# Four attention heads' 32 sample queries on the four quarters of the partitions, with one softmax for the four

## The chip, the cores and the metric

The kernel runs on one core of one Trainium2 chip. The metric is device time in microseconds (us) for one execution of the whole program; a lower time is better.

## What is computed

Two layers of a small model are run over 288 tokens: a prompt of 256 and, apart from it, a sample of 32 new tokens with its own states and caches. Layer 0 mixes tokens by retention and gated linear attention, layer 1 by band attention; each is followed by a gated feed-forward net with a short convolution. Everything is float32. The change is in layer 1's attention, 16 heads of width 128:

```python
def band_attention_prompt(q, k, v, rel_bias):      # chunks of 64 queries
    ...
        s = jnp.einsum('bihd,bjhd->bhij', qn, ks) * scale + bias[None]
        s = jnp.where(valid[None, None, None, :], s, NEG_INF)
        p = jax.nn.softmax(s, axis=-1)
        return jnp.einsum('bhij,bjhd->bihd', p, vs)
...
def band_attention_sample(q, k_new, v_new, k_cache, v_cache, rel_bias):
    ks = jnp.concatenate([k_cache.astype(jnp.float32), k_new], axis=1)
    vs = jnp.concatenate([v_cache.astype(jnp.float32), v_new], axis=1)
    ...
    s = jnp.einsum('bihd,bjhd->bhij', q, ks) * (q.shape[-1] ** -0.5) + bias[None]
    p = jax.nn.softmax(s, axis=-1)
    return jnp.einsum('bhij,bjhd->bihd', p, vs)
```

For each head the sample has 32 queries against 288 keys: 256 from the cache and 32 of its own.

## The kernel before

Activations stand with features on the 128 partitions and the 288 tokens in the columns (256 of the prompt, then 32 of the sample). A projection, `project`, makes one tile of 128 outputs: for each of 16 blocks of 128 inputs it runs three matmuls of 288 columns in float32r (lines 79, 80, 81), since each float32 operand is split into a high and a low part. The weights come in chunks of 8 blocks (512 KB) on SyncE's queue; ScalarE rounds a chunk to its high part `wh` (line 57), VectorE subtracts it to give `wl` (line 58). There are four buffers for a chunk as loaded and three each for `wh` and `wl`.

An attention head is a generator, `att_head`, of five steps:

1. project q and k of the head (two projections);
2. project v;
3. scores and softmax. The prompt's scores take two matmuls (lines 681, 682), the sample's two more with only 32 output partitions (684 against its own keys, 685 against the cache's); v is turned to tokens on partitions by three transposes (689, 690, 691, the last one for the sample). VectorE adds the biases and takes the maxima, ScalarE takes exponentials, VectorE divides; all of it once for each of the prompt's two halves and once for the sample (tile `ass`, 32 partitions by 288);
4. transpose the probabilities: 721, 722, 726 for the prompt, 723, 727, 728 for the sample's cache halves and own keys;
5. the product with v: 734 and 735 for the prompt, 736, 737 and 738 for the sample, all into one PSUM tile, which is split into `bh` and `bl`, the operands of the output projection.

`chain` interleaves the heads: while head h does its steps 4 and 5, head h+1 does 1, 2 and 3, so the instructions of a head's step 5 and of the next head's step 3 stand next to each other on TensorE, after the next head's v projection. Within this order a list scheduler places the instructions; each engine then runs its own list in order. The attention's small loads and stores (caches, biases, k and v out) go through GpSimd's queue (POOL). A plain float32 matmul, such as all those of steps 3 to 5, becomes two instructions on TensorE; a transpose becomes one.

Of the kernel before, what the change touches and what calls it, by code (L numbers as in the profile page):

```python
# [5 lines left out]
F32 = mybir.dt.float32  # L6
F32R = mybir.dt.float32r
U32 = mybir.dt.uint32
AF = mybir.ActivationFunctionType
# [20 lines left out]
NEG = -1e30  # L30
QA, KA, VA, GA, QB, KB, VB, GB = 0, 8, 16, 24, 32, 36, 40, 48


class Trunk:
# [15 lines left out]
    def weights(self, src, n, lo=False):  # L50
        """n k-tiles of 128 rows: the float32 tile as the sum of two float32r tiles."""
        nc = self.nc
        w = self.wp.tile([P, WCH, P], F32, name="w", tag="w", bufs=4)[:, :n, :]
        h = self.wp.tile([P, WCH, P], F32R, name="wh", tag="wh", bufs=3)[:, :n, :]
        l = self.wp.tile([P, WCH, P], F32R, name="wl", tag="wl", bufs=3)[:, :n, :]
        nc.sync.dma_start(w, src)
        nc.scalar.copy(h, w)  # L57
        nc.vector.tensor_tensor(l, w, h.bitcast(F32), op=ALU.subtract)  # L58
        return h, l

    def project(self, src, xh, xl, nk, k0=0, chunks=None, part=None, ps=None):
        """PSUM [128 outputs, T]: the product over nk k-tiles of float32 operands split in two."""
# [20 lines left out]
    def first_project(self, src, x):  # L83
        """As project, while the input is loaded and the first norm's operands come about."""
# [14 lines left out]
    def first_squares(self, x):  # L99
        """The sum of squares, in the place of x."""  # L100
# [16 lines left out]
    def rsqrt(self, out, ms_ps, inv_n, p=P, n=T, tag="rs"):  # L117
        """out = (ms_ps * inv_n + eps) ** -0.5"""
# [37 lines left out]
    def norm_stat(self):  # L156
        """R [128, T]: each token's 1 / rms, on all partitions; worked out with tokens on partitions."""
# [22 lines left out]
    def run(self, ctx):  # L180
# [11 lines left out]
        self.bh = [bp.tile([P, T], F32R, name=f"bh{k}", tag=f"bh{k}") for k in range(KD)]  # L192
        self.bl = [bp.tile([P, T], F32R, name=f"bl{k}", tag=f"bl{k}") for k in range(KD)]
        with self.tc.tile_pool(name="ab", bufs=1) as pool:
            self.ab_mixer(pool, *sums)
        with self.tc.tile_pool(name="x", bufs=1) as xp:
# [7 lines left out]
            with self.tc.tile_pool(name="c", bufs=2) as pool:  # L204
                self.chain(
                    [self.att_head(pool, hd) for hd in range(H_ATT)], 3,
# [31 lines left out]
        # The gate's low-rank features: both parts of the weights side by side in one tile's columns  # L238
        # (their sum is taken in the product with w2, which stands twice).
# [19 lines left out]
    def out_proj(self, w, n, chunks):  # L259
        """x += o @ w, and the next norm's start."""  # L260
# [83 lines left out]
    def head_out(self, pool, o, gates, hd, g):  # L344
        """Gated, normalised head output into the split operands of w_out; o: two PSUM tiles."""
# [18 lines left out]
    def to_tokens(self, pool, feats, name, width, scale=None, bufs=1):  # L364
        """[128 tokens, 3, width] from feature-major [128, T] tiles."""
# [13 lines left out]
    def scaled(self, pool, ps, name, scale=None, rev=False):  # L379
        nc = self.nc  # L380
        z = pool.tile([P, T], F32, name=name, tag=name)
        if scale is None:
            nc.vector.tensor_tensor(z[:, ::-1] if rev else z, ps, self.R, op=ALU.mult)
# [4 lines left out]
    def ab_mixer(self, pool, k0, q0, lo_ps):  # L388
# [19 lines left out]
        def gates():  # L408
            """log sigmoid of the gates, tokens on partitions (its 1/16 is in the level matrices)."""
# [39 lines left out]
    def gla_head(self, pool, hd, w, la, lvl, masks, eyem, hg, first):  # L449
# [14 lines left out]
        # E[:, l]: decays to and from the middle of each token's block of level l. Slot 7: level 256  # L464
        # (tile 0 before, tile 1 behind the middle), and from the sample's start; slot 8: to the end.
# [31 lines left out]
        # Scores, transposed: each pair of tokens belongs to the one level whose middle parts them.  # L497
# [66 lines left out]
        # States.  # L564
# [89 lines left out]

    def att_head(self, pool, hd):
# [4 lines left out]
        kc = pool.tile([P, TP], F32, name="kc", tag="kc")  # L660
        vc = pool.tile([P, 2, P], F32, name="vc", tag="vc")
        nc.gpsimd.dma_start(kc, a["cache_k"][hd])
# [3 lines left out]
        bias_s = pool.tile([TS, T], F32, name="bias_s", tag="bias_s")  # L666
        rel = a["rel"]
        toep = lambda n, m, c: bass.AP(rel.tensor, rel.offset + hd * RELW + c, [[1, n], [1, m]])
        nc.gpsimd.dma_start(bias, toep(P, TP, 256 - 127))
        nc.gpsimd.dma_start(bias_s, toep(TS, T, 256 - 31))  # L670
        nc.gpsimd.memset(bias[:64, :64], NEG)

        q = self.scaled(pool, self.input_product(w[hd]), "aq", scale)
        k = self.scaled(pool, self.input_product(w[16 + hd]), "ak", rev=True)
        nc.gpsimd.dma_start(a["k_out"][hd], k)
        yield
        v = self.scaled(pool, self.input_product(w[32 + hd]), "av", rev=True)
# [3 lines left out]
        nc.tensor.matmul(ps[:, :P], lhsT=q[:, :P], rhs=k[:, TS + P :], start=True, stop=True)  # L681
        nc.tensor.matmul(ps[:, P:384], lhsT=q[:, P:TP], rhs=k[:, TS:], start=True, stop=True)  # L682
        pss = self.mm()[:TS]
# [3 lines left out]
        vt = pool.tile([P, 3, P], F32, name="avt", tag="avt")  # L687
        pv = self.mm()
        nc.tensor.transpose(pv[:, :P], v[:, TS : TS + P], self.ident)
        nc.tensor.transpose(pv[:, P:TP], v[:, TS + P :], self.ident)  # L690
        nc.tensor.transpose(pv[:TS, TP : TP + P], v[:, :TS], self.ident)
        nc.scalar.copy(vt[:, 0:2, :], pv[:, :TP].rearrange("p (t d) -> p t d", t=2))
        nc.scalar.copy(vt[:TS, 2, :], pv[:TS, TP : TP + P])

        s = pool.tile([P, 384], F32, name="as", tag="as")
        ss = pool.tile([TS, T], F32, name="ass", tag="ass")
        mx = pool.tile([P, 3], F32, name="mx", tag="mx")
        sm = pool.tile([P, 3], F32, name="sm", tag="sm")
        nc.vector.memset(mx, 0.0)
        nc.vector.memset(sm, 1.0)  # L700
# [3 lines left out]
        parts = ((s[:, :P], P, 0), (s[:, P:], P, 1), (ss, TS, 2))  # L704
        for x, n, i in parts:
            nc.vector.tensor_reduce(mx[:n, i : i + 1], x, axis=X, op=ALU.max, negate=True)
        for x, n, i in parts:
            nc.scalar.activation(x, x, AF.Exp, bias=mx[:n, i : i + 1], accum_out=sm[:n, i : i + 1])
        nc.vector.reciprocal(sm, sm)
        for x, n, i in parts:  # L710
            nc.vector.tensor_scalar(x, x, sm[:n, i : i + 1], None, op0=ALU.mult)
# [149 lines left out]
```

## Time and profile before

| | us |
|---|---|
| median of three timed runs (2761.59 to 2763.56) | 2762.46 |
| span of the profiled execution, first to last instruction | 2760.1 |
| TensorE busy in that span | 2732.1 (99%) |
| VectorE busy | 1572.3 (57%) |
| ScalarE busy | 1123.9 (41%) |
| GpSimd busy | 126.5 (5%) |

The profile is of one execution, for which the span is given and no other time; the median of the timed runs is 2.4 us longer than that span, and this part lies outside the first and last instruction. Matmuls are pipelined: the duration of one runs from its start to its modelled end and overlaps the next, so what a matmul costs TensorE is read from the distance to the next, which is what the view of the chain that ended last prints.

### The profile page before, as it was taken

Reading aid. Unit: us, or ns where it says so; the run is one execution under the profiler, and the core shown is the slowest. Engines: PE = TensorE matmul, PEld = TensorE weight load, DVE = VectorE, ACT = ScalarE, POOL = GpSimd, SP = SyncE. Lnnn points to the kernel's source line nnn. Section 1 sums busy time; section 2 is a strip of 40 time slices with the busy share of each in tenths; the row PEclk is TensorE's granted clock in tenths of the full one; section 3 lists DMA queues with packets and bytes.
Section 4 is the critical chain, followed back from the end, with each engine's and each line's share of the span. In section 5 each row is a group of like instructions: output and inputs, shape, how many; then the busy total and the mean of one; then the engine's idle time right before and its main releaser. Section 6 shows DMA issues by size and latency. Waiting matters only on the chain.

```text
span 2760.1 us, 49198 instructions
## 1 busy us (share of the span) xinstructions
PE 2732.1 (99%) x20340; PEld 2686.5 (97%) x20340; DVE 1572.3 (57%) x2536; ACT 1123.9 (41%) x1538; POOL 126.5 (5%) x440
## 2 busy tenths in 40 slices
PE   8999999999999999999999999999999999999997
PEld 7999999999999999999999999999999999999997
DVE  6566555666665456665555555556666544666544
ACT  7444343443343333334444333344333333433443
POOL 1000000000000000000011111100000000000000
PEclk9999999999999999999999999999999999999999
DMA  5334444545555555555555555544555555555553
GB/s 198 117 131 142 152 157 149 192 162 166 168 167 161 168 168 165 167 168 162 166 182 170 166 165 165 163 156 162 166 165 166 162 167 168 168 166 166 163 167 125
DMA packets 126546, 448.84 MB, mean 163 GB/s; under 512 B 15562, under 2 KB 15754, under 8 KB 126320
## 3 DMA queue, kind: packets, MB, share of 16 engines
q1 hardware_dynamic: 119520, 427.15, 48.6%
q0 software_dynamic: 6656, 18.49, 2.1%
q8 instruction: 159, 2.61, 0.4%
q14 instruction: 67, 0.55, 0.1%
q10 hardware_dynamic: 144, 0.04, 0.0%
HBM read 435.22 MB, written 10.40 MB: 161 GB/s over the span
## 4 chain that ended last, share of the span: by engine, by line
PE 97%; ACT 1%; DVE 1%; DMA 1%; issue 0%; SPq 0%; DVEq 0%; ACTq 0%
PE acc L80 31%; PE acc L79 30%; PE acc L81 30%; PE mm L520 1%; DMA x_in<-in_xT 0%; PE mm L372 0%; PE mm L643 0%; ACT wh L57 0%; PE mm L682 0%; PE mm L685 0%; PE mm L734 0%; PE mm L681 0%; DVE wl L58 0%; DVE y L334 0%; PE mm L738 0%
## 5 line engine op out<-in xcount | busy, mean ns | idle before, releaser
L57 ACT CAST wh<-w 128x1024 fp32r<-128x1024 f32 (+1 forms) x816 | 843.7, 1034 | 1505.9 <-PE acc L80 1209.0
L58 DVE TENSOR_TENSOR wl<-w,wh 128x1024 fp32r<-128x1024 f32 (+1 forms) x816 | 981.0, 1203 | 761.7 <-ACT wh L57 761.4
L79 PE MATMUL acc<-xh,wh 128*128 128x288 f32 x4480 | 1323.0, 295 | 8.6 <-ACT wh L57 7.7
L81 PE MATMUL acc<-xh,wl 128*128 128x288 f32 x4480 | 1323.5, 295 | 1.3 <-DVE wl L58 1.3
L80 PE MATMUL acc<-xl,wh 128*128 128x288 f32 x4480 | 1324.0, 296 | 0.0
L79 PEld LDWEIGHTS acc<-xh,wh 128*128 128x128 f32 x4480 | 843.2, 188 | 13.3 <-ACT wh L57 7.9
L81 PEld LDWEIGHTS acc<-xh,wl 128*128 128x128 f32 x4480 | 842.6, 188 | 2.8 <-DVE wl L58 2.1
L80 PEld LDWEIGHTS acc<-xl,wh 128*128 128x128 f32 x4480 | 843.0, 188 | 2.0 <-issue 1.0
L79 PE MATMUL acc<-bh,wh 128*128 128x288 f32 x1920 | 567.1, 296 | 0.4 <-ACT wh L57 0.4
L80 PE MATMUL acc<-bl,wh 128*128 128x288 f32 x1920 | 566.3, 295 | 0.0
L81 PE MATMUL acc<-bh,wl 128*128 128x288 f32 x1920 | 565.0, 294 | 0.0
L79 PEld LDWEIGHTS acc<-bh,wh 128*128 128x128 f32 x1920 | 360.1, 188 | 1.3 <-ACT wh L57 0.6
L81 PEld LDWEIGHTS acc<-bh,wl 128*128 128x128 f32 x1920 | 361.2, 188 | 0.0
L80 PEld LDWEIGHTS acc<-bl,wh 128*128 128x128 f32 x1920 | 360.3, 188 | 0.1
L298 DVE SCALAR_TENSOR_TENSOR gc<-gp,convp,gc 128x290 f32<-128x290 f32 x176 | 91.3, 519 | 3.2
L304 DVE TENSOR_TENSOR v<-acc,R 128x288 f32<-128x288 f32 x88 | 40.3, 458 | 87.8 <-PE acc L81 87.8
L289 DVE TENSOR_TENSOR gp<-acc,R 128x256 f32<-128x256 f32 x88 | 37.5, 426 | 88.3 <-PE acc L81 88.3
L291 POOL COPY conv_out<-gp 128x2 f32<-128x2 f32 x88 | 16.4, 187 | 1312.7 <-DVE gp L289 1312.7
L114 ACT CAST bh<-v 128x288 fp32r<-128x288 f32 x88 | 38.1, 433 | 15.3 <-DVE v L306 15.3
L296 DVE TENSOR_SCALAR gc<-gp,convp 128x290 f32<-128x290 f32 x88 | 38.0, 432 | 9.5
L305 DVE TENSOR_TENSOR v<-v,sg 128x256 f32<-128x256 f32 x88 | 37.5, 426 | 9.9 <-DVE v L304 0.9
L115 DVE TENSOR_TENSOR bl<-v,bh 128x288 fp32r<-128x288 f32 x88 | 39.8, 452 | 0.7 <-ACT bh L114 0.7
(256 smaller groups left out, 1188.2 us busy)
## 6 DMA issues: line engine op xcount, KB each, us to landing
w<-in_w_ffn_up SPq DMA_DIRECT2D x352, 512.0 KB, 3.7
w<-in_w_ffn_down SPq DMA_DIRECT2D x128, 512.0 KB, 3.7
w<-in_w_in SPq DMA_DIRECT2D x112, 512.0 KB, 3.8
w<-in_w_qkv SPq DMA_DIRECT2D x96, 512.0 KB, 3.9
w<-in_w_ffn_down SPq DMA_DIRECT2D x64, 384.0 KB, 3.2
w<-in_w_out_ab SPq DMA_DIRECT2D x32, 512.0 KB, 3.8
w<-in_w_out_att SPq DMA_DIRECT2D x32, 512.0 KB, 3.8
x<-in_xT SPq DMA_DIRECT2D x4, 576.0 KB, 6.1
```

What stands on the lines that cost most here:

```text
L57: nc.scalar.copy(h, w)
L58: nc.vector.tensor_tensor(l, w, h.bitcast(F32), op=ALU.subtract)
L79: nc.tensor.matmul(ps, lhsT=h, rhs=xh, start=first, stop=False)
L80: nc.tensor.matmul(ps, lhsT=h, rhs=xl, start=False, stop=False)
L81: nc.tensor.matmul(ps, lhsT=l, rhs=xh, start=False, stop=last)
L114: self.nc.scalar.copy(h, v)
L115: self.nc.vector.tensor_tensor(l, v, h.bitcast(F32), op=ALU.subtract)
L289: nc.vector.tensor_tensor(gp[:, 2 : TP + 2], g[:, :TP], self.R[:, :TP], op=ALU.mult)
L296: nc.vector.tensor_scalar(gc, gp[:, 0:W], cw[:, 0:1], cw[:, 3:4], op0=ALU.mult, op1=ALU.add)
L298: nc.vector.scalar_tensor_tensor(gc, gp[:, w : w + W], cw[:, w : w + 1], gc, op0=ALU.mult, op1=ALU.add)
L304: nc.vector.tensor_tensor(v, u, self.R, op=ALU.mult)
L305: nc.vector.tensor_tensor(v[:, :TP], v[:, :TP], s[:, :TP], op=ALU.mult)
```

## The change

The heads are taken in groups of four (GRP). A head keeps only the prompt's part in its steps; its q, its k (own and cached keys now side by side in one tile of 544 columns) and its cached values are kept until the group's fourth head, in eight buffers. The fourth head carries a second generator, `att_sample`, which does the sample's part for the four heads at once: head i's 32 queries stand on partitions 32i to 32i+31. There the scores of each head are one matmul of 288 columns into its quarter of a PSUM tile; bias, maximum and exponential are one instruction each for the 128 rows. The own keys' probabilities are spread into a block-diagonal 128 by 128 matrix (by `bd`, a constant of ones and zeros), so that one matmul multiplies all four heads' own values; the cached values take eight matmuls, four quarters by two halves. The division by the sum comes after the product, and one transpose of the result gives features on partitions. The sample's columns of four heads' `bh` and `bl` are then written by one instruction each, for which the 16 tiles are made one tile `bh_all` with 16 slices. The outputs for the sample's v leave from a tile of their own.

```diff
+GRP = P // TS
+KEPT = 2 * GRP
...
-        self.bh = [bp.tile([P, T], F32R, name=f"bh{k}", tag=f"bh{k}") for k in range(KD)]
...
+        self.bh_all = bp.tile([P, KD, T], F32R, name="bh", tag="bh")
...
+        self.bh = [self.bh_all[:, k, :] for k in range(KD)]
...
+    def reversed(self, ps, prompt, sample):
...
+        nc.vector.tensor_tensor(prompt[:, ::-1], ps[:, :TP], self.R[:, :TP], op=ALU.mult)
+        nc.vector.tensor_tensor(sample[:, ::-1], ps[:, TP:], self.R[:, TP:], op=ALU.mult)
...
+                last = self.att_sample(pool, g, kept, v4, bd) if i == GRP - 1 else iter(())
+                heads.append(self.att_head(pool, g * GRP + i, kept, v4, last))
...
+        k = pool.tile([P, T + TP], F32, name="ak", tag="ak", bufs=KEPT)
+        vc = pool.tile([P, 2, P], F32, name="vc", tag="vc", bufs=KEPT)
+        nc.gpsimd.dma_start(k[:, T:], a["cache_k"][hd])
...
-        nc.gpsimd.dma_start(bias_s, toep(TS, T, 256 - 31))
...
-        k = self.scaled(pool, self.input_product(w[16 + hd]), "ak", rev=True)
...
+        self.reversed(self.input_product(w[16 + hd]), k[:, :TP], k[:, TP:T])
...
-        nc.tensor.matmul(pss[:, :TS], lhsT=q[:, TP:], rhs=k[:, :TS], start=True, stop=True)
-        nc.tensor.matmul(pss[:, TS:T], lhsT=q[:, TP:], rhs=kc, start=True, stop=True)
...
-        nc.tensor.transpose(pv[:TS, TP : TP + P], v[:, :TS], self.ident)
...
-        nc.vector.tensor_tensor(ss, pss[:, :T], bias_s, op=ALU.add)
...
+        next(sample, None)
...
-        nc.tensor.transpose(ps[:, TP:T], ss[:, TS + P :], small)
...
+        nc.tensor.transpose(ps[:, TP:384], s[:, P:TP], self.ident)
...
-        nc.tensor.transpose(ps[:, P : P + TS], ss[:, TS : TS + P], small)
-        nc.tensor.transpose(ps[:TS, P + TS : P + 2 * TS], ss[:, :TS], small)
...
+        po = self.mm()[:, :TP]
+        nc.tensor.matmul(po, lhsT=vt[:, 1, :], rhs=p0, start=True, stop=False)
+        nc.tensor.matmul(po[:, P:], lhsT=vt[:, 0, :], rhs=p1, start=False, stop=True)
...
-        nc.tensor.matmul(po[:, TP:], lhsT=vc[:, 1, :], rhs=p0[:, TP:], start=True, stop=False)
-        nc.tensor.matmul(po[:, TP:], lhsT=vc[:, 0, :], rhs=p1[:, P:], start=False, stop=False)
-        nc.tensor.matmul(po[:, TP:], lhsT=vt[:TS, 2, :], rhs=p2, start=False, stop=True)
...
+    def att_sample(self, pool, g, kept, v4, bd):
...
+        nc.gpsimd.dma_start(bias, bass.AP(rel.tensor, at, [[RELW, GRP], [1, TS], [1, T]]))
+        nc.gpsimd.dma_start(a["v_out_s"][g], v4[0])
+        ps = self.mm()[:, :T]
+        for c, (q, k, _) in zip(quarter, kept):
+            nc.tensor.matmul(ps[c], lhsT=q[:, TP:], rhs=k[:, TP:], start=True, stop=True)
+        pv = self.mm()[:, :P]
+        nc.tensor.transpose(pv, v4[0].rearrange("p h t -> p (h t)"), self.ident)
...
+        nc.scalar.copy(vt, pv)
...
+        nc.vector.tensor_tensor(s, ps, bias, op=ALU.add)
+        nc.vector.tensor_reduce(mx, s, axis=mybir.AxisListType.X, op=ALU.max, negate=True)
+        nc.scalar.activation(s, s, AF.Exp, bias=mx, accum_out=sm)
...
+        nc.vector.tensor_tensor(
+            own,
+            s[:, None, :TS].to_broadcast([P, GRP, TS]),
+            bd[:, :, None].to_broadcast([P, GRP, TS]),
+            op=ALU.mult,
+        )
+        nc.vector.reciprocal(sm, sm)
+        yield
...
+        nc.tensor.transpose(ps[:, :P], own.rearrange("p h t -> p (h t)"), self.ident)
+        for i in range(2):
+            nc.tensor.transpose(ps[:, (i + 1) * P : (i + 2) * P], s[:, TS + i * P : TS + (i + 1) * P], self.ident)
...
+        nc.scalar.copy(pT, ps[:, :384].rearrange("p (t q) -> p t q", t=3))
+        yield
+        po = self.mm()[:, :P]
+        nc.tensor.matmul(po, lhsT=pT[:, 0, :], rhs=vt, start=True, stop=False, skip_group_check=True)
+        for i in range(2):
+            for c, (_, _, vc) in zip(quarter, kept):
+                nc.tensor.matmul(
+                    po[c], lhsT=pT[:, 1 + i, c], rhs=vc[:, i, :], start=False, stop=i == 1, skip_group_check=True
+                )
...
+        nc.vector.tensor_scalar(o, po, sm, None, op0=ALU.mult)
+        yield
...
+        nc.tensor.transpose(ps, o, self.ident)
```

What this does to TensorE's list is seen at two places. The first is the seam between two heads, where one head's product with v is followed by the next head's scores. In the kernel before, TensorE's list has there (`ap` and `as` are probabilities of the prompt, `aq` and `ak` the queries and keys, `av` the values, `kc` and `vc` the caches; the last figure is the output's partitions by columns):

```order
L734 MATMUL mm<-ap_15766,avt 128x256
L735 MATMUL mm<-ap_15767,avt 128x128
L736 MATMUL mm<-ap_15766,vc 128x32
L737 MATMUL mm<-ap_15767,vc 128x32
L738 MATMUL mm<-ap_15768,avt 128x32
L681 MATMUL mm<-ak,aq 128x128
L682 MATMUL mm<-ak,aq 128x256
L684 MATMUL mm<-ak,aq 32x32
L685 MATMUL mm<-kc,aq 32x256
L689 MATMUL mm<-ident,av 128x128
L690 MATMUL mm<-ident,av 128x128
L691 MATMUL mm<-ident,av 32x128
```

In the changed kernel the same seam between two heads of a group is

```order
L742 MATMUL mm<-ap_15702,avt 128x256
L743 MATMUL mm<-ap_15703,avt 128x128
L705 MATMUL mm<-ak,aq 128x128
L706 MATMUL mm<-ak,aq 128x256
L710 MATMUL mm<-ident,av 128x128
L711 MATMUL mm<-ident,av 128x128
```

Six of twelve rows are gone: the sample's three products, its two score matmuls and its transpose. At the fourth head's scores the group's own rows follow, the four score matmuls and the transpose of the four heads' values (`av_15250`):

```order
L705 MATMUL mm<-ak,aq 128x128
L706 MATMUL mm<-ak,aq 128x256
L710 MATMUL mm<-ident,av 128x128
L711 MATMUL mm<-ident,av 128x128
L760 MATMUL mm<-ak,aq 32x288 x4
L762 MATMUL mm<-ident,av_15250 128x128
```

The second place is the seam after a group's fourth head, where its products with v stand ahead of the next group's first scores, and the transpose of the result (`ao`) a few rows behind them, between rows of the next projection:

```order
L789 MATMUL mm<-avt_16042,ap_16199 128x128
L792 MATMUL mm<-vc,ap_16199 32x128 x8
L705 MATMUL mm<-ak,aq 128x128
L706 MATMUL mm<-ak,aq 128x256
L710 MATMUL mm<-ident,av 128x128
L711 MATMUL mm<-ident,av 128x128
L81 MATMUL acc<-xh_70,wh 128x288
L82 MATMUL acc<-xl_86,wh 128x288
L83 MATMUL acc<-xh_70,wl 128x288
L81 MATMUL acc<-xh_71,wh 128x288
L82 MATMUL acc<-xl_87,wh 128x288
L799 MATMUL mm<-ident,ao_16282 128x128
```

Between a product with v and its transpose, where the division by VectorE lies, the scheduler has put nine rows of other work. On VectorE's list the same seam reads

```order
L60 TENSOR_TENSOR wl<-w,wh 128x1024
L117 TENSOR_TENSOR bl<-mm,bh 128x256
L796 TENSOR_SCALAR ao_17254<-mm,sm_17019 128x128
L716 TENSOR_TENSOR as<-mm,bias 128x128
L717 TENSOR_TENSOR as<-mm,bias 128x256
L720 TENSOR_REDUCE mx<-as 128x1 x2
L117 TENSOR_TENSOR bl<-mm,bh 128x4x32
```

with the division (line 796) ahead of the next head's softmax.

## Rows read from the trace of the kernel before

**Rows 1.** The page: busy time of TensorE, and from its picture of the span in 40 slices the clock that TensorE was granted, in tenths.

```profile
PE 2732.1 (99%) x20340; PEld 2686.5 (97%) x20340; DVE 1572.3 (57%) x2536; ACT 1123.9 (41%) x1538; POOL 126.5 (5%) x440
...
PEclk9999999999999999999999999999999999999999
```

**Rows 2.** The page, the chain of work that ended last, by engine.

```profile
PE 97%; ACT 1%; DVE 1%; DMA 1%; issue 0%; SPq 0%; DVEq 0%; ACTq 0%
```

**Rows 3.** Who TensorE's matmuls waited for in the whole span: total us, times, longest us. These are the four longest.

```profile
PE acc L79 <- ACT wh L57: 8.1, 3, 7.1
PE mm L175 <- DVE rd L172: 2.9, 2, 1.6
PE mm L471 <- ACT E L477: 1.6, 4, 1.0
PE acc L81 <- DVE wl L58: 1.3, 3, 0.7
```

**Rows 4.** Busy time by engine in the stretch from the first head's scores to the last one's, with the granted clock (PEclk, 1.00 is 2.4 GHz), the DMA engines' busy share and GB/s.

```profile
1444.90:1796.30 351.40, 351.40 (x2570) 332.35 (x2570) 179.50 (x329) 140.00 (x272) 48.98 (x101) 1.00 0.53 166
```

**Rows 5.** The chain in order of time: the first and the last of the 16 heads' score matmuls against the cache (start us, us, what).

```profile
1445.99 0.43 PE mm L685 x2
...
1796.89 0.43 PE mm L685 x2
```

**Rows 6.** The chain at the first head's scores, before which only a projection stands.

```profile
1445.15 0.22 PE mm L681 x2
1445.37 0.43 PE mm L682 x2
```

**Rows 7.** The chain at the seam between the first and the second head (from a projection's last row to the next one's first two). Each row's us is what it adds to the chain.

```profile
1466.87 0.13 PE acc L81
1467.00 0.43 PE mm L734 x2
1467.43 0.22 PE mm L735 x2
1467.65 0.14 PE mm L736 x2
1467.80 0.22 PE mm L737 x2
1468.02 0.33 PE mm L738 x2
1468.35 0.42 PE mm L681 x2
1468.77 0.43 PE mm L682 x2
1469.20 0.18 PE mm L684 x2
1469.38 0.43 PE mm L685 x2
1469.82 0.26 PE mm L689
1470.08 0.11 PE mm L690
1470.19 0.11 PE mm L691
1470.30 0.14 PE acc L79
```

**Rows 8.** The chain at the transposes of the second head's probabilities.

```profile
1482.99 0.11 PE mm L721
1483.10 0.11 PE mm L722
1483.21 0.18 PE mm L723
1483.39 0.26 PE mm L726
1483.65 0.17 PE mm L727
1483.82 0.03 PE mm L728
1483.85 0.33 PE acc L79
1484.18 0.13 PE acc L80
```

**Rows 9.** The timeline of VectorE and of ScalarE behind that seam: weight chunks and the sample's exponential (start us, us, engine, line, operation, and in brackets the idle time before it).

```profile
1467.98 1.23 DVE L58 TENSOR_TENSOR wl<-w,wh 128x1024 fp32r<-128x1024 f32 x1 [0.49 <-ACT wh L57]
...
1474.51 1.23 DVE L58 TENSOR_TENSOR wl<-w,wh 128x1024 fp32r<-128x1024 f32 x1 [1.06 <-ACT wh L57]
...
1471.65 0.52 ACT L708 ACTIVATE ass<-ass,mx 32x288 f32<-32x288 f32 x1
...
1473.42 1.05 ACT L57 CAST wh<-w 128x1024 fp32r<-128x1024 f32 x1 [1.16 <-issue]
```

**Rows 10.** Groups of VectorE's instructions in the attention, by line and shape: times, then busy us and mean ns of one.

```profile
L703 DVE TENSOR_TENSOR ass<-mm,bias_s 32x288 f32<-32x288 f32 x16 | 7.0, 436 | 0.0
L706 DVE TENSOR_REDUCE mx<-ass 32x1 f32<-32x288 f32 x16 | 6.9, 430 | 0.0
L711 DVE TENSOR_SCALAR as<-as,sm 128x128 f32<-128x128 f32 x16 | 4.6, 286 | 0.4
```

**Rows 11.** The DMA issues: KB each, and the median us from issue to landing.

```profile
bias_s<-in_rel POOLq DMA_DIRECT2D x16, 36.0 KB, 3.8
```

More of the change, by code (lines that the diff above doesn't have):

```diff
@@ L205, in run @@
                 self.chain(
-                    [self.att_head(pool, hd) for hd in range(H_ATT)], 3,
+                    self.att_heads(pool), 3,
                     lambda: self.out_start(a["w_out_att"], (0, WCH)),
@@ L651, in ret_head, with att_heads, att_head @@
         self.head_out(pool, o, z, hd, hg[:, 0, :])
-    def att_head(self, pool, hd):
+    def att_heads(self, pool):
+        bd = self._one(pool, "bd", [P, GRP], self.a["bd"])
+        heads = []
+        for g in range(H_ATT // GRP):
+            v4 = []
+            kept = []
+            for i in range(GRP):
+                last = self.att_sample(pool, g, kept, v4, bd) if i == GRP - 1 else iter(())
+                heads.append(self.att_head(pool, g * GRP + i, kept, v4, last))
+        return heads
+    def att_head(self, pool, hd, kept, v4, sample):
         nc, a = self.nc, self.a
@@ L705, in att_head @@
[L705 to L708, printed above, removed]
+        parts = ((s[:, :P], 0), (s[:, P:], 1))
+        for x, i in parts:
+            nc.vector.tensor_reduce(mx[:, i : i + 1], x, axis=X, op=ALU.max, negate=True)
+        for x, i in parts:
+            nc.scalar.activation(x, x, AF.Exp, bias=mx[:, i : i + 1], accum_out=sm[:, i : i + 1])
@@ L719, in att_head @@
+        p1 = pool.tile([P, P], F32, name="ap1", tag="ap1")
         ps = self.mm()
[L720 removed]
         nc.tensor.transpose(ps[:, :P], s[:, :P], self.ident)
         nc.tensor.transpose(ps[:, P:TP], s[:, TP:384], self.ident)
[L723 to L727 removed]
@@ L737, in att_head @@
-        nc.tensor.matmul(po[:, TP:], lhsT=vc[:, 0, :], rhs=p1[:, P:], start=False, stop=False)
-        nc.tensor.matmul(po[:, TP:], lhsT=vt[:TS, 2, :], rhs=p2, start=False, stop=True)
-        self.split(self.bh[hd], self.bl[hd], po)
+        nc.tensor.transpose(ps[:, TP:384], s[:, P:TP], self.ident)
+        nc.scalar.copy(p0, ps[:, :TP])
+        nc.scalar.copy(p1, ps[:, TP:384])
+        next(sample, None)
+        yield
+        po = self.mm()[:, :TP]
+        nc.tensor.matmul(po, lhsT=vt[:, 1, :], rhs=p0, start=True, stop=False)
@@ new lines, in att_head @@
+        nc.tensor.matmul(po[:, P:], lhsT=vt[:, 0, :], rhs=p1, start=False, stop=True)
+        self.split(self.bh[hd][:, :TP], self.bl[hd][:, :TP], po)
+        next(sample, None)
+        yield
+        next(sample, None)
+    def att_sample(self, pool, g, kept, v4, bd):
+        nc, a = self.nc, self.a
+        quarter = [slice(i * TS, (i + 1) * TS) for i in range(GRP)]
+        bias = pool.tile([P, T], F32, name="bias_s", tag="bias_s")
+        rel = a["rel"]
+        at = rel.offset + g * GRP * RELW + 256 - 31
+        nc.gpsimd.dma_start(bias, bass.AP(rel.tensor, at, [[RELW, GRP], [1, TS], [1, T]]))
[5 more added lines that the diff above has]
+        nc.tensor.transpose(pv, v4[0].rearrange("p h t -> p (h t)"), self.ident)
+        vt = pool.tile([P, P], F32, name="avt4", tag="avt4")
+        nc.scalar.copy(vt, pv)
+        s = pool.tile([P, T], F32, name="as4", tag="as4")
+        own = pool.tile([P, GRP, TS], F32, name="own4", tag="own4")
+        mx = pool.tile([P, 1], F32, name="mx4", tag="mx4")
+        sm = pool.tile([P, 1], F32, name="sm4", tag="sm4")
+        nc.vector.tensor_tensor(s, ps, bias, op=ALU.add)
[9 more added lines that the diff above has]
+        yield
+        ps = self.mm()
+        nc.tensor.transpose(ps[:, :P], own.rearrange("p h t -> p (h t)"), self.ident)
+        for i in range(2):
+            nc.tensor.transpose(ps[:, (i + 1) * P : (i + 2) * P], s[:, TS + i * P : TS + (i + 1) * P], self.ident)
+        pT = pool.tile([P, 3, P], F32, name="ap4", tag="ap4")
+        nc.scalar.copy(pT, ps[:, :384].rearrange("p (t q) -> p t q", t=3))
+        yield
+        po = self.mm()[:, :P]
[5 more added lines that the diff above has]
+                )
+        o = pool.tile([P, P], F32, name="ao4", tag="ao4")
+        nc.vector.tensor_scalar(o, po, sm, None, op0=ALU.mult)
+        yield
+        ps = self.mm()[:, :P]
+        nc.tensor.transpose(ps, o, self.ident)
+        heads = slice(g * GRP, (g + 1) * GRP)
+        self.split(
+            self.bh_all[:, heads, TP:], self.bl_all[:, heads, TP:], ps.rearrange("p (h t) -> p h t", h=GRP)
+        )
@@ L795 @@
     "k_out": (H_ATT, P, T),
-    "v_out": (H_ATT, P, T),
+    "v_out": (H_ATT, P, TP),
+    "v_out_s": (H_ATT // GRP, P, GRP, TS),
     "conv_out": (P, 2, NF, 4),
```

76 lines of the change are left out of this document (32 added, 44 removed).

## The prediction

> **What bounds the kernel now.** I read the page's busy times and clock first, then the chain that ended last, then who TensorE waited for, then the attention's stretch, and last the chain row by row at two seams. TensorE is busy 99% of the span and its granted clock is in the top tenth in every slice [rows 1]; the chain runs over TensorE for 97% [rows 2]. Its longest sums of waiting are 8.1, 2.9, 1.6 and 1.3 us in the whole span [rows 3], and in the 351.4 us from the first head's scores to the last one's there is none: busy 351.40 of 351.40, at clock 1.00, while VectorE is busy 179.5, ScalarE 140.0, and DMA 0.53 [rows 4]. So a microsecond taken from TensorE's list in the attention is a microsecond of the span, as long as the other engines keep up, and what they save is worth nothing by itself.
>
> The 16 heads follow each other at (1796.89 - 1445.99) / 15 = 23.39 us [rows 5]. Of it three projections take 3 x 48 matmuls at 0.1325 us, 19.08 us (the chain prints 0.13 or 0.14 [rows 7]). The other 4.3 us are the two seams, and the chain shows what each row adds. The reader is to see there that tiny matmuls with 32 columns cost nearly as much as the large ones, and that a row behind one of another shape pays extra: the score matmul 681 adds 0.22 behind a projection [rows 6] but 0.42 behind the 32-row matmul 738; the transpose 689 adds 0.26 where its like, 690, adds 0.11 [rows 7].
>
> **What is removed.** At the seam between heads the prompt's own rows cost 0.43 (734) + 0.22 (735) + 0.22 (681, its price without the change of shape) + 0.43 (682) + 0.11 + 0.11 (two transposes) = 1.52 us. The seam takes 1470.30 - 1467.00 = 3.30 us [rows 7]. So the sample's rows there, with the changes of shape they cause, cost 1.78 us. At the transposes of the probabilities the six rows take 1483.85 - 1482.99 = 0.86 us, and the next projection's first row adds 0.33 where 0.13 is normal, 0.20 more [rows 8]; three full transposes at 0.11 are 0.33, so the sample costs 0.86 - 0.33 + 0.20 = 0.73 us. Together 2.51 us a head, **40.2 us** for 16.
>
> **What is added**, per group of four heads, all on TensorE. A matmul of 128 columns is 0.22, of 256 columns 0.43 [rows 7], so 288 columns are 0.49. Going into the 32-output shape: 684 and its second instruction add 0.18 where 32 columns stream in 2 x 0.027, so 0.13 extra; coming out: 689's 0.15 extra.
> - Scores (760): 4 x 0.49 + 0.13 = 2.07. Transpose of the values (762): 0.11 + 0.15 = 0.26.
> - Three transposes beside the head's own (782, 784): 0.33.
> - Products with v: 0.22 for the block-diagonal one (789), 8 x 0.22 + 0.13 = 1.89 for the cached values (792), and 0.15 on the row behind them.
> - Transpose of the result (799): 0.11.
>
> The sum is 5.03 us, **20.1 us** for four groups. This counts the four quarters one after the other, as 684 and 685, the nearest rows (32 outputs, neighbours in the list), do: 685 adds its full 0.43. No row before has matmuls for different quarters next to each other, so the price is bounded: from above by each paying a change of shape of its own, from below by the four quarters running wholly together. I take the serial price, by the nearest row, and keep both ends for the range.
>
> **The other engines.** VectorE drops per head the 32-row add (0.44), maximum (0.43), a division of about 0.35 and two memsets, and gets two extra 32-column products (for k and v), below the 0.29 of a 128-column row; a group adds one 288-column add and maximum, a masked copy, a reciprocal and the division 796, each of the size of [rows 10]. That is less work than before and is worth nothing, since VectorE is idle half of this stretch [rows 4].
>
> What must not happen is that weights come late. Behind the seam the next cast of a chunk starts at 1473.42, 3.1 us after the projection's first row at 1470.30 [rows 7, 9]: this is when TensorE empties the first of three buffers (24 x 0.1325 = 3.18 us), not when the softmax is done. Its second half ends at 1474.51 + 1.23 = 1475.74 [rows 9], and TensorE needs it when all three chunks are used, at 1470.30 + 9.54 = 1479.84: 4.1 us of slack. In the changed kernel the group's exponential (0.52 us [rows 9]) follows its last score matmul by an add and a maximum of 0.44 and 0.43, about 1.6 us in all, still ahead of that cast. The division 796 has nine rows of cover, 0.15 + 0.22 + 0.43 + 0.22 + 5 x 0.13 = 1.7 us, against about 0.29 plus the passing on; without that cover it would cost some 0.5 us a group.
>
> At the end of the attention no further head gives cover: product, division, transpose and split follow each other with only a few rows between. Between nothing (the same stretch before shows no wait) and 1 us; I take **0.3 us**.
>
> Sum: 40.2 - 20.1 - 0.3 = 19.8 us less. From the profiled span of 2760.1 that is 2740.3; the timed median lies 2.4 above this span and that part stays, so **2742.7 us**, 0.72% less. The arithmetic on two seams of 0.01 us rows carries about 2 us either way.
>
> **The rivals.**
> 1. *The quarters run beside each other.* The four score matmuls write different quarters of the output, and so do those with the cached values. Each is two instructions, and the second of one quarter must follow the first; but the first of the next quarter might run beside it. Then the scores take (4 + 1) instead of 8 half steps of 0.24, 0.73 less, and the cached values 9 instead of 16 of 0.11, 0.77 less: 1.50 a group, 6.0 in all, **2736.7 us**. Wholly together they would take 0.49 and 2 x 0.22, 2.8 less a group, **2731.6 us**. For it: the seams are bound by TensorE alone [rows 4], so nothing else would hide it. Against it: 685 behind 684 pays in full [rows 7], though both are for the same quarter.
>
>    The Trainium skill, TensorE: Matmul & The Clock Gate, section "Part 3: Packing small matmuls — row/col tiling", says that matmuls in different 32-column tiles of the array run concurrently and gives 2.38 times the speed for three; no run here shows that, and an estimate by its 3.07 for four tiles in rows would take 2.5 us from a group, 2732.7 us.
> 2. *Each quarter drains the engine.* If going from one quarter to the next costs like a change of shape, the ten steps inside a group's two runs pay 0.13 each or even 0.28: 5.2 to 11.2 us in all, **2748 to 2754 us**. For it: both known changes of shape cost [rows 7, 8]. Against it: the shape does not change there.
>
>    The Trainium skill, TensorEngine Tiling (Array Packing), section "Tiling Modes", says that a change of the mode drains the engine and a change of the tile within a mode does not; the trace agrees with the first half by the 0.15 to 0.20 extra above, and by the second half this rival falls.
> 3. *A wait behind the group's softmax makes it slower.* VectorE and ScalarE run their lists in order, so the casts of weights stand behind the group's exponential, which needs the group's bias, and TensorE stands behind the casts. The price is what that exponential is late beyond the 1.6 us until the next cast and the 4.1 us of slack. It decides from (19.8 + 5.5) / 4 = 6.3 us of stall a group, which is an exponential about 12 us late: 2768 us and more. For it: the load takes 3.8 us from issue [rows 11] and is issued in order behind other work of POOL. Against it: in the changed list it stands a whole group ahead, some 80 us.
> 4. *It does not shorten TensorE's list*, because a group's rows cost as much as four heads' sample rows, 10.05 instead of 5.03. Half of the price before is extra for shapes and for full loads of 128 columns at 32 columns of work, and both are paid once instead of four times, so I give it little.
>
> **How the numbers follow.** What a measurement of this kernel tells from no change is about 0.2%, 5.5 us. Serial: 0.47, its own range 2739 to 2746. Rival 1: 0.35 for pairs and 0.07 for wholly together. Rival 2: 0.05. Rival 3: 0.03. Rival 4: 0.03. The range goes from the wholly concurrent end to rival 2's cheaper end, 2731 to 2748, and leaves out little more than a tenth beside errors of size. Faster by over 0.2% hold serial, rival 1 and rival 2: 0.94. The same: rival 4, 0.03. Slower: 0.03.
>
> **What would show it.** In the chain of the changed kernel a seam inside a group takes 1.5 us and the transposes 0.33, with 0.13 on the row behind, and three of four heads follow at 19.08 + 1.85 = 20.9 us. The four rows 760 add about 2.07 us together (serial), 1.3 (pairs), or 0.6; the eight rows 792 about 1.9, 1.1 or 0.6: this decides between the forecast and rivals 1 and 2. TensorE shows no waits in the stretch; waits for `wh` or `wl`, or of ScalarE for the group's maximum, would be rival 3. The prediction is wrong if ordinary seams do not shrink to 1.85 us, or if TensorE idles there.

## The result, and the profile after

The changed kernel takes **2732.5 us** (median; 2732.1 to 2733.3) against 2762.1 us of the kernel before, timed beside it: a ratio of 0.989, 95% interval 0.9878 to 0.9902. It is 1.1% faster. The forecast was 0.72% less, 2742.7 us; the measured time is 10.2 us below it, inside the range and at its lower end, where rival 1's "wholly together" stood with 2731.6 us. (Of the 2.4 us between span and median that the forecast added, some 0.6 isn't time outside the span: the profiled execution of the changed kernel took 2732.17 us with a span of 2730.4, 1.8 us apart, and the runs of the kernel before that list both lie as far apart.)

The page of the changed kernel (busy times, granted clock, chain by engine) answers to [rows 1, 2]:

```profile
PE 2702.9 (99%) x20240; PEld 2670.8 (98%) x20240; DVE 1562.7 (57%) x2512; ACT 1117.4 (41%) x1494; POOL 123.2 (5%) x433
...
PEclk9999999999999999999999999999999999999999
...
PE 97%; ACT 1%; DVE 1%; DMA 1%; issue 0%; SPq 0%; DVEq 0%; ACTq 0%
```

TensorE is still the bound, at the same clock, and its list is shorter: 29.2 us less busy time in a span that is 2760.1 - 2730.4 = 29.7 us shorter. The four longest waits are those of [rows 3] (the first of them here), and none of them lies in the attention:

```profile
PE acc L81 <- ACT wh L59: 8.2, 3, 7.1
```

Lines 742 and 743 are the head's own products now, 705 and 706 its scores, 710 and 711 the two transposes of its values. First the distance of two heads inside a group, read from the chain at line 706 (start us, us, what); it answers to [rows 5]:

```profile
1466.29 0.43 PE mm L706 x2
...
1487.18 0.43 PE mm L706 x2
```

20.89 us in place of 23.39. The chain at the first seam of a group's last head, where the group's scores (760) and the transpose of its values (762) stand, answers to [rows 7]:

```profile
1507.20 0.43 PE mm L742 x2
1507.63 0.22 PE mm L743 x2
1507.85 0.22 PE mm L705 x2
1508.08 0.43 PE mm L706 x2
1508.51 0.11 PE mm L710
1508.62 0.11 PE mm L711
1508.73 0.62 PE mm L760 x8
1509.35 0.26 PE mm L762
1509.61 0.14 PE acc L81
```

The upper six rows sum to 1.52 us, the price of an ordinary seam. The row to look at is 760: four matmuls of 288 columns, each of two instructions, add 0.62 us, where the forecast had 2.07. Next the chain at the transposes of the probabilities, the head's own three and the group's (782, 784); it answers to [rows 8]:

```profile
1522.52 0.11 PE mm L735
1522.63 0.11 PE mm L782
1522.74 0.22 PE mm L784 x2
1522.96 0.13 PE acc L81
```

All of one shape, and the projection's row behind them pays nothing extra. Last the chain at the group's product with v:

```profile
1529.96 0.22 PE mm L789 x2
1530.18 0.57 PE mm L792 x16
1530.76 0.42 PE mm L705 x2
...
1532.49 0.11 PE mm L799
```

Eight matmuls (792) add 0.57 us where the forecast had 1.89, and the next head's scores, 0.42 for 0.22, pay 0.20 to come out of the 32-output shape.

So a group costs 0.62 + 0.26 + 0.33 + 0.22 + 0.57 + 0.20 + 0.11 = 2.31 us, not 5.03. At the end of the attention, where no further head gives cover, three rows of the chain are longer than their like elsewhere:

```profile
1775.05 0.70 PE mm L742 x2
...
1776.77 0.33 PE acc L83
...
1777.99 0.50 PE acc L81 x2
```

742 waits 0.27 us for its probabilities (0.70 against 0.43), and 81 some 0.23 for the group's result (0.50 for two rows of 0.13 or 0.14): 0.5 us. (Only the 0.23 turns out to be the group's, by an experiment below. The 0.33 is the way out of the shape, counted above.) The sum of the chain is 40.2 - 4 x 2.31 - 0.5 = 30.5 us; the span shows 29.7.

### The profile page after: what moved, and what is told of

Same layout as the page of the kernel before. It is cut to its first block, busy times and chain, and to the rows that moved or that the text cites. A ratio compares the mean times of both kernels' runs of the same rounds, so it can differ in the third digit from the quotient of the medians.

```text
span 2730.4 us, 48893 instructions
## 1 busy us (share of the span) xinstructions
PE 2702.9 (99%) x20240; PEld 2670.8 (98%) x20240; DVE 1562.7 (57%) x2512; ACT 1117.4 (41%) x1494; POOL 123.2 (5%) x433
## 4 chain that ended last, share of the span: by engine, by line
PE 97%; ACT 1%; DVE 1%; DMA 1%; issue 0%; SPq 0%; DVEq 0%; ACTq 0%
PE acc L82 31%; PE acc L83 31%; PE acc L81 31%; PE mm L530 1%; DMA x_in<-in_xT 0%; PE mm L376 0%; PE mm L653 0%; ACT wh L59 0%; PE mm L742 0%; PE mm L706 0%; DVE wl L60 0%; DVE y L338 0%; DMA w<-in_w_in 0%; ACT L487 0%; PE mm L654 0%
```

## The experiments

The theory after the result: matmuls whose outputs lie on different quarters of the partitions run beside each other, all four, and this is the whole of the miss. Rivals: only neighbours overlap, so the order in which they are written decides; something else was cheaper than counted and the quarters' rows are short for another reason; the group's softmax has a price that the chain hides.

### Do all four quarters run together?

Five rounds of score matmuls instead of one, quarter by quarter in turn:

```diff
-        for c, (q, k, _) in zip(quarter, kept):
-            nc.tensor.matmul(ps[c], lhsT=q[:, TP:], rhs=k[:, TP:], start=True, stop=True)
+        for _ in range(5):
+            for c, (q, k, _) in zip(quarter, kept):
+                nc.tensor.matmul(ps[c], lhsT=q[:, TP:], rhs=k[:, TP:], start=True, stop=True)
```

> Of the changed kernel, with the four score matmuls of a group issued five times over, round by round (quarter 0, 1, 2, 3, 0, 1, ...): 16 matmuls more in each of the four groups, which write the same scores again. Theory 'together' (the four quarters of the array run beside each other, as the 0.62 us for four in the chain of the changed kernel says): a round costs one matmul of 288 columns, some 0.49 us, so 4 x 0.49 = 1.95 us per group, 7.8 us in all, 2740.3 us. Theory 'one after the other' (the prediction's price): 16 x 0.49 = 7.8 us per group, 31 us in all, 2763.9 us. Theory 'pairs' (only the two instructions that stand next to each other overlap): 16 us, 2748 us.

Measured: 2740.8 us (ratio to before 0.9923, 0.9908 to 0.9938), 8.3 us above the changed kernel, where "together" said 7.8. In its chain the 20 matmuls of a group stand as one piece:

```profile
1509.32 2.56 PE mm L761 x40
```

(2.56 - 0.62) / 4 = 0.485 us for a further round of four: what one matmul of 288 columns alone was worked out to cost (0.43 x 288 / 256 = 0.49). "Pairs" and "one after the other" fall. The timeline of the changed kernel at the instant 1508.66 says the same from the other side: four instructions of line 760 are under way within 0.45 us.

```profile
1508.66 0.45 PE L760 MATMUL mm<-ak,aq 128*32 128x288 f32 x4
```

Their starts in the trace are 7 ns apart, and the second instructions of the four follow 0.27 us later, again 7 ns apart.

### Does the order in which they are written matter?

The prediction's "pairs" rested on a picture of the order: the second instruction of a quarter must follow its first, so only what stands next in the list can run beside it. Two kernels test that. The first exchanges the two loops around the cached values:

```diff
-        for i in range(2):
-            for c, (_, _, vc) in zip(quarter, kept):
+        for c, (_, _, vc) in zip(quarter, kept):
+            for i in range(2):
```

> Of the changed kernel, with the two loops around the product with the cached values exchanged: the two matmuls of quarter 0, then the two of quarter 1, and so on; nothing else differs. Theory 'a free quarter goes ahead': no change, 2732.5 us within 0.2%, and the piece of the chain for line 792 stays at 0.57 us. Theory 'in program order': a quarter's four instructions of 0.11 us follow one another and the next quarter starts with the last of them, so 13 x 0.11 + 0.13 = 1.5 us in place of 0.57, about 0.95 us per group, 3.8 us in all, 2736.3 us.

Measured: 2732.7 us (2732.4 to 2732.9), no change, and its piece of the chain is hardly longer:

```profile
1531.05 0.59 PE mm L792 x16
```

So four instructions in a row for one quarter don't hold up the next quarter's. The second kernel puts ten in a row:

```diff
-            nc.tensor.matmul(ps[c], lhsT=q[:, TP:], rhs=k[:, TP:], start=True, stop=True)
+            for _ in range(5):
+                nc.tensor.matmul(ps[c], lhsT=q[:, TP:], rhs=k[:, TP:], start=True, stop=True)
```

> The same 16 matmuls more per group, but with each quarter's five in a row (quarter 0 five times, then quarter 1 five times, ...), so that neighbours in the program need the same quarter. Theory 'a free quarter goes ahead' (what is behind a matmul that waits for its quarter may overtake it): as in the other order, some 2740 us. Theory 'in program order': a quarter's first can start only after the last of the quarter ahead of it has started, so a group takes 17 matmuls of 0.49 us, 8.3 us in place of 0.62, 7.7 us more per group, 31 us in all, 2763 us. A time between the two would mean that the engine looks ahead over some matmuls but not over five.

Measured: 2758.9 us (ratio to before 0.9986, 0.9977 to 0.9996): 26.4 us more than the changed kernel, between the two theories. The same 20 matmuls that took 2.56 us in turns now take 7.00:

```profile
1508.79 7.00 PE mm L761 x40
```

The starts in the trace tell why. Within a quarter they lie 0.2425 us apart, after a first step of 0.267; the first instruction of a quarter is the only one of 430 or 431 ns, the others have 406. Quarter 0 and the beginning of quarter 1:

```
quarter 0: 1508.721 1508.988 1509.231 1509.473 1509.716 1509.958 1510.201 1510.443 1510.686 1510.928
quarter 1: 1510.206 1510.474 1510.716 1510.959 ...
```

Which quarter a record belongs to is not written in it; it is read from this rhythm, from the 430 ns, and from the semaphores: in each quarter only the first weight load waits for one, and only the last matmul signals. The instruction at 1510.928, the last of quarter 0, is one that signals, and quarter 1's first, at 1510.206, whose weight load waits for a semaphore of its own, started 0.72 us ahead of it. Quarter 1 starts 5 ns behind the seventh instruction of quarter 0, with the eighth to tenth still to come: matmuls that stand later in the program overtake three that wait for their quarter, and not a fourth. By this rule pv_quarter's four in a row (one starts, three wait) are just within reach. There the first instructions of the four quarters start at 1530.981, 1530.995, 1531.008 and 1531.021, all before any quarter's second (1531.115), so the last of them overtakes nine, three of each quarter ahead of it: the limit counts for each quarter, not in all. The rule makes a forecast for six in a row, so that was run too:

```diff
+            for _ in range(3):
```

> As dup_quarter, with three score matmuls in a row for each quarter in place of five (8 more per group). It tells how far the engine looks ahead: in dup_quarter an instruction started 0.2425 us after the one ahead of it in its quarter, and the next quarter's first started right behind the seventh of ten, 6 x 0.2425 + 0.03 = 1.49 us after the quarter's own first. Theory 'three may stand waiting and the fourth passes' (six instructions a quarter, so the next quarter starts behind the third): a step of 2 x 0.2425 + 0.03 = 0.515 us per quarter, the piece 3 x 0.515 + 6 x 0.2425 + 0.13 = 3.13 us in place of 0.62, 10.0 us in all, 2742.6 us. Theory 'in program order, with only the last one overlapped': 21 x 0.2425 + 0.13 = 5.2 us, 18.4 us in all, 2750.9 us. Theory 'any free quarter goes ahead up to some six instructions': 6 x 0.2425 + 0.13 = 1.6 us, 3.9 us in all, 2736.4 us.

Measured: 2742.4 us (ratio 0.9928, 0.9912 to 0.9945), where "three may stand waiting" said 2742.6 and the other two 2750.9 and 2736.4. The piece was to be 3.13 us:

```profile
1509.74 3.12 PE mm L761 x24
```

The Trainium skill, TensorE: Matmul & The Clock Gate, section "Part 3: Packing small matmuls — row/col tiling", says that matmuls in different tiles of the array run concurrently; this trace agrees (0.485 us for a round of four). The same section says that matmuls start and end in program order; here they don't, by the starts above, and the measurement decides.

### What does the whole group cost?

The group's scores, softmax and products go; what stays is the store of its values:

```diff
-        ps = self.mm()[:, :T]
-        for c, (q, k, _) in zip(quarter, kept):
...
+        heads = slice(g * GRP, (g + 1) * GRP)
+        nc.gpsimd.memset(self.bh_all[:, heads, TP:].bitcast(F32), 0.0)
+        nc.gpsimd.memset(self.bl_all[:, heads, TP:].bitcast(F32), 0.0)
```

> The changed kernel without the sample's scores, softmax and product: the sample's columns of the attention output are filled with zeros by GpSimd, and its bias isn't loaded. That prices the whole group. Theory 'the chain's pieces are all of it' (0.62 + 0.26 + 0.33 + 0.22 + 0.57 + 0.20 + 0.11 = 2.31 us per group and 0.5 us at the end): 9.7 us less than the changed kernel, 2722.8 us. By the prediction's serial price (5.03 us per group): 20 us less, 2712 us. If the group's softmax on VectorE and ScalarE also delayed something that the chain doesn't show under its lines: more than 9.7 us less.

Measured: 2723.8 us (ratio 0.9859, 0.9842 to 0.9875), 8.7 us below the changed kernel, where the chain's pieces said 9.7 and the serial price 20. Of the 9.7, the 0.27 that 742 waits at the end of the attention isn't the group's: without the group the row is as long, behind a cast of weights on ScalarE that stands ahead of the head's own probabilities (between these two rows the chain has the copy 736):

```profile
1766.41 1.05 ACT wh L59
...
1767.79 0.70 PE mm L742 x2
```

So the pieces that the edit takes away sum to 9.5 us. By stage the traces agree better: from the first head's scores to the last head's own product it takes 322.24 us in place of 330.13, and from there to TensorE's end 941.84 in place of 943.31, together 9.36 us (from the starts of the instructions); the stretch ahead of the attention, which the edit doesn't touch, was 0.63 us longer in this profile. So the traces show no price of the group beyond the chain's pieces: with it, the changed kernel has 9 us left in the sample's attention, of the 40.2 us that the kernel before had in it.

### Does the group's softmax hold up the weights?

This probes rival 3's slack. One long ScalarE copy stands behind the group's exponential, then three of them (`range(3)` in place of `range(1)`):

```diff
         nc.scalar.activation(s, s, AF.Exp, bias=mx, accum_out=sm)
+        late = pool.tile([P, 16, 256], mybir.dt.bfloat16, name="late", tag="late", bufs=1)
+        for _ in range(1):
+            nc.scalar.copy(late, s[:, None, :256].to_broadcast([P, 16, 256]))
```

> The changed kernel with one ScalarE copy of 4096 columns (at the cast's 1.05 us for 1024 columns some 4.2 us) right behind each group's exponential, written to a tile that nothing reads. It stands in front of the cast of the next weights, as the group's own exponential does (0.54 + 0.19 us). Theory 'slack': the casts run two tiles ahead of TensorE (a tile is 3.17 us of it), so cast and subtraction may come 6.34 - 1.05 - 1.23 = 4.0 us later without a wait; the cast is delayed by 3.8 us, so no change, 2732.5 us within 0.2%. Theory 'ScalarE's block is waited for' (rival 3, with the slack of 1.6 us alone): (4.2 - 1.6) x 4 = 10 us more, 2743 us.

Measured: 2732.4 us (2731.8 to 2732.5), no change. In the first three groups TensorE's list is the same as in the changed kernel; at the last one the scheduler put more rows of the projection between the group's steps, so the run tells of the seams alone. The timeline of ScalarE behind the first group's exponential, in the changed kernel

```profile
1512.74 1.05 ACT L59 CAST wh<-w 128x1024 fp32r<-128x1024 f32 x1 [0.43 <-ACT as L771]
```

and with one copy

```profile
1513.31 3.61 ACT L774 CAST late<-as 128x4096 bf16<-128x4096 f32 x1
1516.82 2.00 ACT L59 CAST wh<-w 128x1024 fp32r<-128x1024 f32 x2
```

The copy took 3.61 us, not 4.2. In the changed kernel the cast behind the exponential starts at 1512.74; here the group stands 0.98 us later in the span, so the cast is 16.82 - 0.98 - 12.74 = 3.1 us late, and nobody waits. At least 3.1 of the 4.1 us of slack that the prediction read are there.

> The same with three such copies in each group, with one cast of weights between the first and the second and one between the second and the third: 12.6 us of ScalarE in a stretch of 12.7 us in which it also has four casts. Theory 'slack': the second cast comes some 5.8 us late and the third some 8 us, 4.0 us are free, so PE waits about 4 us per group (the first wait some 1.8 us, the second the rest), 16 us in all, 2748 us; the waits should stand as PE's waits for wl and wh of lines 59 and 60. If nothing waits even then, ScalarE has more room than the buffers say.

Measured: 2741.1 us (ratio 0.9923, 0.991 to 0.9937), 8.6 us more where "slack" said 16, and for another reason than expected. In the first three groups TensorE waits for nothing, but its list isn't the same there: with the copies in the program, the scheduler put the products 742 to 795 behind 24 rows of the projection instead of 48, so those groups don't measure the slack. All of the loss is in the last group, which no further head covers. Its chain leaves TensorE and goes over ScalarE, through the copies that stand ahead of the probabilities:

```profile
1775.98 3.51 ACT late L774
1779.48 0.27 ACT ap L736
1779.75 3.51 ACT late L774
1783.26 0.17 ACT ap L737
1783.47 0.59 PE mm L743 x2
```

Behind the wait TensorE runs at half its clock for a while, as the table of stretches shows (us; busy us and instructions of PE, PEld, DVE, ACT, POOL; PEclk; DMA share; GB/s):

```profile
1778.00:1783.40 5.40, 1.64 (x10) 1.01 (x8) 0.00 (x0) 5.40 (x5) 0.00 (x0) 1.00 0.29 97
...
1788.00:1790.00 2.00, 2.00 (x10) 2.00 (x10) 0.00 (x0) 0.00 (x0) 0.57 (x4) 0.50 0.69 184
```

and the chain there has 0.24 us a row:

```profile
1788.20 0.24 PE acc L81
```

So at the seams a cast that is 3.1 us late costs nothing; where ScalarE was made late enough to cost time, it was at the end of the attention, and by the head's probabilities, not by the weights of rival 3.

### Is it the change of shape that the sample's rows paid for?

The prediction took 0.13 us for going into a 32-wide shape and 0.15 to 0.20 for coming out, from rows that could also be read as small matmuls being dear. In the kernel **before**, only the order of the transposes is changed:

```diff
+        ps1 = self.mm()
...
+        nc.tensor.transpose(ps1[:, :P], s[:, P:TP], self.ident)
         nc.tensor.transpose(ps[:, TP:T], ss[:, TS + P :], small)
+        nc.tensor.transpose(ps1[:, P : P + TS], ss[:, TS : TS + P], small)
+        nc.tensor.transpose(ps1[:TS, P + TS : P + 2 * TS], ss[:, :TS], small)
...
-        ps = self.mm()
-        nc.tensor.transpose(ps[:, :P], s[:, P:TP], self.ident)
-        nc.tensor.transpose(ps[:, P : P + TS], ss[:, TS : TS + P], small)
-        nc.tensor.transpose(ps[:TS, P + TS : P + 2 * TS], ss[:, :TS], small)
```

> The kernel before, with the six transposes after each head's softmax in another order: the three of 128x128 first, then the three that have 32 rows or columns, instead of large and small in turn. No operation is added or removed. Theory 'a change of the matmul's shape on the array costs time of its own' (0.13 us into it and 0.15 to 0.20 us out of it, as the pieces of the chain at the seam of the kernel before and after suggest): one change in and out less per head, some 0.25 us x 16 = 4 us less, 2758 us. Theory 'the small ones are dear by themselves': no change, 2762 us.

Measured: 2758.7 us against 2763.2 of the kernel before beside it, ratio 0.9986 (0.9977 to 0.9995): 4.4 us less (1.4 to 6.4 by the interval), where 4 was expected for changes of shape and nothing for dear small ones. Its chain, against [rows 8]:

```profile
1482.60 0.11 PE mm L722
...
1482.93 0.17 PE mm L725
1483.10 0.06 PE mm L726
1483.16 0.03 PE mm L727
1483.19 0.33 PE acc L79
```

The six transposes take 1483.19 - 1482.60 = 0.59 us in place of 0.86, and 0.27 x 16 = 4.3 us. The same was then done in layer 0 of the **changed** kernel, whose retention and linear-attention heads also multiply over the sample's 32 rows between large products:

```diff
-        for i in range(2):
-            c = slice(i * P, (i + 1) * P)
-            po = self.mm()[:, :T]
+        pos = [self.mm()[:, :T] for _ in range(2)]
+        cs = [slice(i * P, (i + 1) * P) for i in range(2)]
+        for po, c in zip(pos, cs):
...
-            nc.tensor.matmul(po[:, TP:], lhsT=vt[:TS, 2, c], rhs=pT[:TS, 384:], start=True, stop=False)
...
+        for po, c in zip(pos, cs):
+            nc.tensor.matmul(po[:, TP:], lhsT=vt[:TS, 2, c], rhs=pT[:TS, 384:], start=False, stop=True)
```

> The changed kernel, with the same thing done in layer 0: in each of the eight heads there, the products that contract over the sample's 32 rows stand behind the two large ones of both halves instead of between them (the lines 639 to 644, 653 to 655 and 566 to 569). No operation is added or removed. Theory 'a change of shape costs time of its own': the second halves' large products lose the 0.08 to 0.11 us that they take longer than the first halves' (0.51 against 0.43, 1.06 against 0.95 us), and one change in falls away per pair, some 0.15 us each: 0.5 us x 4 + 0.25 us x 4 = 3 us less, 2729.5 us. Theory 'dear by themselves': no change, 2732.5 us.

Measured: **2727.8 us** (2727.3 to 2728.5), ratio to before 0.9874 (0.986 to 0.9887). That is 4.7 us below the changed kernel (2732.1 to 2733.3), where 3 was expected for changes of shape, and the fastest of all; wide1, timed beside it, took 2732.4. In the changed kernel the chain at a retention head's second half reads

```profile
292.72 0.33 PE mm L641 x2
293.05 0.56 PE mm L643 x4
293.61 0.95 PE mm L653 x4
294.56 0.62 PE mm L654 x2
295.18 1.06 PE mm L653 x4
296.24 0.62 PE mm L654 x2
```

and with the 32-row products together (641 is the old 639, 644 the old 643, 646 the old 641 of both halves, 656 and 658 the old 653 and 654)

```profile
290.56 0.51 PE mm L641 x2
...
291.30 0.37 PE mm L644 x4
291.67 0.56 PE mm L646 x4
292.22 1.92 PE mm L656 x8
294.14 1.06 PE mm L658 x4
```

654 goes from 2 x 0.62 to 1.06 us. The gain that the expectation lacked is in 643: the same four matmuls cost 0.37 us behind a large product and 0.56 behind a 32-row one. By the starts in the two traces the regrouped rows of a retention head lose 0.78 us on average and those of a linear-attention head 0.37 (expected were 0.5 and 0.25), 4.6 us in all. One part of the expectation failed: the second half's first large product was to fall from 0.51 to 0.43 us and still adds 0.51, now behind 32-column matmuls over all 128 rows. So not all of the extra is a change to or from 32 rows; what this part is, no run here shows. The Trainium skill, TensorEngine Tiling (Array Packing), section "Tiling Modes", says that a change of the tiling mode drains the engine; both pairs of kernels agree that changing back and forth costs time, by 0.27 us a head in the one and 4.7 us in all in the other.

## Why the prediction came out as it did

- **What bounds the kernel:** right. TensorE stayed at 99%, without a wait between the groups, and the span fell by what its list lost (29.2 us of busy time, 29.7 of span).
- **What is removed:** right in size. 2.51 us a head were worked out, and the distance of two heads fell from 23.39 to 20.89; an ordinary seam takes the 1.52 us of the prediction, and the row behind the transposes its 0.13.
- **What is added:** this step was wrong in two of its terms. Line 762 (0.26), 782 and 784 (0.33), 789 (0.22) and 799 (0.11) came out to the hundredth. The scores (760) were put at 2.07 and took 0.62; the cached values with the row behind them at 2.04 and took 0.57 + 0.20. Together 5.03 against 2.31 a group, 10.9 us over four groups. 19.8 + 10.9 - 0.2 is 30.5, and the span shows 29.7; where the other 0.8 went isn't shown; it is of the size in which two profiles of an untouched stretch differ (0.63 above).
- **Why they were wrong:** "I take the serial price, by the nearest row". That row was 685 behind 684 [rows 7], and both have the same quarter, so it could not bear on matmuls of different quarters; the prediction said so itself and chose it all the same. The measured price lies between the two bounds (0.1 us a group above the lower one, 2.8 us less), so the bounds were right and the choice between them was not. That the time lies in the range at all is owed to the lower bound, which was given 0.07, and not to the sum.
- **Rival 1:** its mechanism is what happened, in the form given 0.07. "Pairs", given 0.35, took for granted that instructions start in the order of the program. dup_quarter and dup_quarter3 show that they don't.
- **The end of the attention:** 0.3 us was taken, for product, division, transpose and split without cover; that way costs 0.23 (81 behind 799). The 0.27 of line 742 was not foreseen: there a cast of weights stands on ScalarE ahead of the head's own probabilities, with or without the group (no_sample).
- **Rival 2:** falls. A step from one quarter to the next costs 7 ns of start.
- **Rival 3:** falls. No wait for weights lies in the attention, and wide1 shows at least 3.1 us of slack at the seams.
- **Rival 4:** falls; the list got shorter by 29.2 us.

## What to carry to other kernels

Where a bound has two ends far apart and the nearest row doesn't have the property that decides between them, the choice is not made by nearness; the chances are to be spread over both ends. Small matmuls of several heads that fit on different quarters of the output's partitions cost little more here than one of them (0.62 us for four where one is 0.49; the other 0.13 is what going into the shape was priced at), when they follow each other in the program; turn by turn is the safe order, since a fourth instruction that waits for the same quarter held up all that stood behind it. Small and large shapes are best kept apart in the list: putting 32-row products side by side gave 4 to 5 us here twice, with no operation saved.

## What was not expected of the hardware

Matmuls of a free quarter overtake earlier ones in the program that wait for theirs: three for each quarter, not four (7.00 us for 20 matmuls in blocks of five, 3.12 for 12 in blocks of three, 2.56 for 20 in turns), and nine in all in pv_quarter. So TensorE doesn't run its own list strictly in order, as the section on the kernel before has it of each engine. And after 5.4 us in which TensorE was busy for 1.64, its granted clock fell from 1.00 to 0.50, which is 1.2 GHz, and the projection's matmuls then took 0.24 us each in place of 0.13.
